# The first load of a layernorm kernel, in one transfer or in three transfers over interleaved partitions

## The chip, the cores and the metric

The kernel runs on one core of a Trainium2 chip. The metric is the time of one execution on the device, in microseconds.

## The reference

```python
z = x + residual                       # (16, 1024, 512) float32
mean = np.mean(z, axis=-1, keepdims=True)
var = np.var(z, axis=-1, keepdims=True)
z_norm = (z - mean) / np.sqrt(var + eps)
out = gamma * z_norm + beta
```

That is 33.5 MB of x, 33.5 MB of the residual and 33.5 MB of output: 100.7 MB through the core's DMA engines, and little arithmetic for each byte.

## The kernel before

Rows of 512 numbers are spread over 128 partitions. A written plan gives the order of the transfers, all issued from SyncE: `x0+8` loads rows 0 to 7 of each partition, `r` is the residual, `o` a store.

```python
PLAN = """
x0+8 r0+8 x8+8 r8+8 x16+16 r16+16 x32+16 r32+16 x48+16
o0+16 r48+16 ...
"""
EARLY = 2
...
    def move(out, in_, s):
        i = nc.sync.dma_start(out=out, in_=in_).then_inc(s, 16)
        if len(first) < EARLY:
            first.append(i.ins)
...
        if kind == "x":
            # (cut: waits for stores, once the buffer is used again)
            move(part(zbuf, Z_ROWS, lo, n), dram(xf, lo, n), sx[loads_x.index((lo, n))])
...
                nc.gpsimd.wait_ge(s[landed[key]], 16)      # GpSimd, ahead of each add
```

At the end of the program the instructions in `first` are moved ahead of the barrier with which all engines begin. So the first two loads, x0 and r0, are issued at once and everything else after the barrier. GpSimd adds, ScalarE takes mean and variance, VectorE normalizes, SyncE stores.

Of the kernel before, what the change touches and what calls it, by code (L numbers as in the profile page):

```python
# [14 lines left out]
Z_ROWS = 64  # L15
# [16 lines left out]
Z_TURNS = Z_ROWS // TURN  # L32


EARLY = 2


@with_exitstack
def kernel(
# [9 lines left out]
    nc = tc.nc  # L49
    P = nc.NUM_PARTITIONS  # L50
    xf = x.flatten_outer_dims()
# [16 lines left out]
    def of_kind(kind):  # L68
        found = [(lo, n) for k, lo, n in moves if k == kind]
        assert sum(n for _, n in found) == total  # L70
        return found

    def dram(t, lo, n):

        b0 = lo - lo % BLOCK
        v = t[P * b0 : P * (b0 + BLOCK), :].rearrange("(p j) d -> p j d", p=P)
        return v[:, lo - b0 : lo - b0 + n, :].rearrange("p a b -> p (a b)")

    zbuf = nc.alloc_sbuf_tensor("zbuf", [P, Z_ROWS * D], FP32)
# [17 lines left out]
    def sem(name):  # L97
        s = nc.alloc_semaphore(name)
        sems.append(s)
        return s  # L100

    loads_x, loads_r, stores = of_kind("x"), of_kind("r"), of_kind("o")
    sx = [sem(f"sx{c}") for c in range(len(loads_x))]
# [13 lines left out]
    def part(buf, size, lo, n):  # L117
        assert lo % size + n <= size
        return buf[:, (lo % size) * D : (lo % size + n) * D]
# [17 lines left out]
    first = []  # L137

    def move(out, in_, s):
        i = nc.sync.dma_start(out=out, in_=in_).then_inc(s, 16)  # L140
        if len(first) < EARLY:
            first.append(i.ins)

    gone = 0
    for kind, lo, n in moves:
        if kind == "x":
            while gone < len(stores) and stores[gone][0] < lo + n - Z_ROWS:
                nc.sync.wait_ge(so[gone], 16)
                gone += 1
            move(part(zbuf, Z_ROWS, lo, n), dram(xf, lo, n), sx[loads_x.index((lo, n))])  # L150
        elif kind == "r":
            if lo + n > R_ROWS:
                last = (lo + n - R_ROWS) // TURN - 1
                nc.sync.wait_ge(s_rstd[last % Z_TURNS], last // Z_TURNS + 1)
            move(part(rbuf, R_ROWS, lo, n), dram(rf, lo, n), sr[loads_r.index((lo, n))])
        else:
            if lo + n > seen:
                nc.sync.wait_ge(s_out, lo + n)
                seen = lo + n
            move(dram(of, lo, n), part(zbuf, Z_ROWS, lo, n), so[stores.index((lo, n))])  # L160
# [9 lines left out]
    landed = {"x": 0, "r": 0}  # L170
    lo = 0
    for n in ADDS:
        for key, loads, s in (("x", loads_x, sx), ("r", loads_r, sr)):
            while landed[key] < len(loads) and loads[landed[key]][0] < lo + n:
                nc.gpsimd.wait_ge(s[landed[key]], 16)  # L175
                landed[key] += 1
        z = part(rbuf, R_ROWS, lo, n)
        nc.gpsimd.tensor_tensor(  # L178
            out=z, in0=part(zbuf, Z_ROWS, lo, n), in1=z, op=ALU.add
        ).then_inc(s_sum[lo // TURN % R_TURNS], 1)  # L180
        lo += n
# [131 lines left out]
```

## Time and profile before

| | before |
|---|---|
| time, median of the first 3 runs | 238.48 us |
| span of the profiled run | 236.7 us |
| busy: DMA queue of SyncE / ScalarE / VectorE / GpSimd | 99.4% / 78% / 75% / 61% |
| first issue, first packets | 0.00 us; 1.02 to 1.49 us |
| first add on GpSimd | 12.29 us |

Read the table from its third row down: one queue is busy all the time. The lines behind it are in the prediction.

### The profile page before, as it was taken

How to read it: one execution, taken by the hardware profiler on the slowest of the kernel's cores; microseconds unless marked ns; L12 is line 12 of the kernel's file. 1: busy time of each engine (PE TensorE's matmuls, PEld its weight loads, DVE VectorE, ACT ScalarE, POOL GpSimd, SP SyncE). 2: the span in 40 equal slices, each digit the busy share in tenths (PEclk: the TensorE clock that was granted, in tenths of full speed). 3: DMA queues.
4: the chain of work that ended last, by engine and by line, in shares of the span. 5: the costliest groups of instructions: out<-in, count | busy, mean ns of one | idle time of the engine just before them, and what ended most of it. 6: DMA issues, size and time to landing. Idle time of an engine off the chain costs nothing.

```text
span 236.7 us, 1000 instructions
## 1 busy us (share of the span) xinstructions
PE 3.8 (2%) x4; PEld 1.2 (0%) x4; DVE 177.2 (75%) x290; ACT 183.8 (78%) x545; POOL 144.0 (61%) x36
## 2 busy tenths in 40 slices
PE   0600000000000000000000000000000000000000
PEld 0100000000000000000000000000000000000000
DVE  0001999629999999599980999809999999999950
ACT  2019997299999996999909998099999999999600
POOL 0098920999799307993079920899799798800000
DMA  8999999999999999999999999999999999999997
GB/s 310 443 426 432 426 443 443 443 443 443 410 388 443 443 443 432 426 393 432 443 443 443 443 438 421 415 421 432 429 424 435 426 432 440 439 432 443 438 390 324
DMA packets 4469, 100.68 MB, mean 425 GB/s; under 512 B 498, under 2 KB 498, under 8 KB 500
## 3 DMA queue, kind: packets, MB, share of 16 engines
q1 hardware_dynamic: 4464, 100.67, 99.4%
q14 instruction: 1, 0.01, 0.0%
q10 hardware_dynamic: 4, 0.00, 0.0%
HBM read 67.11 MB, written 33.55 MB: 425 GB/s over the span
## 4 chain that ended last, share of the span: by engine, by line
ACT 48%; DMA 35%; POOL 6%; DVE 4%; issue 1%; SPq 1%; ACTq 0%; DVEq 0%; POOLq 0%
DMA rbuf<-in_residual_dram 35%; ACT junk_s L211 25%; ACT junk_m L201 21%; POOL rbuf L178 6%; DVE zbuf L239 3%; ACT std L220 2%; DVE zbuf L253 1%; SPq L140 1%; DVE rstd L247 0%; ACTq L194 0%; DVEq L231 0%; POOLq L175 0%; ACTq L199 0%; ACTq L195 0%
## 5 line engine op out<-in xcount | busy, mean ns | idle before, releaser
L178 POOL TENSOR_TENSOR rbuf<-zbuf,rbuf 128x2048 f32<-128x2048 f32 x32 | 143.7, 4521 | 62.2 <-DMA rbuf<-in_residual_dram 60.0
L239 DVE SCALAR_TENSOR_TENSOR zbuf<-rbuf,nm,gamma_p 128x512 f32<-128x512 f32 x128 | 87.1, 743 | 47.8 <-ACT std L220 47.8
L201 ACT ACTIVATE junk_m<-rbuf 128x512 f32<-128x512 f32 x128 | 74.2, 580 | 34.0 <-POOL rbuf L178 33.7
L211 ACT ACTIVATE junk_s<-rbuf,nm 128x512 f32<-128x512 f32 x128 | 88.8, 694 | 1.0
L253 DVE SCALAR_TENSOR_TENSOR zbuf<-zbuf,rstd,beta_p 128x512 f32<-128x512 f32 x128 | 87.1, 744 | 1.1
L211 ACT ACTIVATION_READ_ACCUMULATOR junk_s<-rbuf,nm 128x1 f32 x128 | 23.9, 187 | 0.0
L201 ACT ACTIVATION_READ_ACCUMULATOR junk_m<-rbuf 128x1 f32 x128 | 23.8, 186 | 0.0
L220 ACT ACTIVATE std<-ssq,eps_t 128x4 f32<-128x4 f32 x32 | 9.5, 297 | 1.0
L247 DVE RECIPROCAL rstd<-std 128x4 f32<-128x4 f32 x32 | 5.5, 171 | 0.0
L192 ACT ACT_TABLE_LOAD x1 | 1.3, 1283 | 2.7 <-PEq L60 2.7
L131 PE MATMUL gamma_p<-gb_row,ones 1*128 1x512 f32 x2 | 2.0, 1122 | 6.6 <-DMA gb_row<-in_gamma_dram 6.6
L131 PE MATMUL beta_p<-gb_row,ones 1*128 1x512 f32 x2 | 1.9, 1056 | 0.0
L126 DVE MEMSET ones<- 1x128 f32 x1 | 0.2, 165 | 2.0 <-PEq L60 2.0
L131 PEld LDWEIGHTS beta_p<-gb_row,ones 1*128 1x128 f32 x2 | 0.7, 332 | 1.0 <-DMA gb_row<-in_beta_dram 0.5
L131 PEld LDWEIGHTS gamma_p<-gb_row,ones 1*128 1x128 f32 x2 | 0.5, 306 | 6.6 <-issue 6.6
L294 POOL MEMSET const-float32-0.0<- 128x1 f32 x1 | 0.1, 98 | 0.2 <-issue 0.2
L294 POOL MEMSET const-bfloat16-1.0<- 128x1 bf16 x1 | 0.1, 101 | 0.0
L294 POOL MEMSET const-uint8-127<- 128x1 uint8 x1 | 0.1, 101 | 0.0
L294 POOL MEMSET const-float32-1.0<- 128x1 f32 x1 | 0.1, 98 | 0.0
L127 DVE MEMSET eps_t<- 128x1 f32 x1 | 0.1, 59 | 0.0
## 6 DMA issues: line engine op xcount, KB each, us to landing
zbuf<-in_x_dram SPq DMA_DIRECT2D x6, 4096.0 KB, 28.9
rbuf<-in_residual_dram SPq DMA_DIRECT2D x6, 4096.0 KB, 21.2
out_dram<-zbuf SPq DMA_DIRECT2D x6, 4096.0 KB, 31.0
zbuf<-in_x_dram SPq DMA_DIRECT2D x4, 2048.0 KB, 14.9
rbuf<-in_residual_dram SPq DMA_DIRECT2D x4, 2048.0 KB, 14.0
out_dram<-zbuf SPq DMA_DIRECT2D x3, 2048.0 KB, 22.5
out_dram<-zbuf SPq DMA_DIRECT2D x2, 1024.0 KB, 10.0
gb_row<-in_gamma_dram ACTq DMA_DIRECT2D x1, 2.0 KB
```

The lines of the kernel that those rows point to most:

```text
L126: nc.vector.memset(ones[:, :], 1.0).then_inc(s_const, 1)
L131: nc.tensor.matmul(dest[:, :], ones[:, :], gb_row[:, k * D : (k + 1) * D], start=True, stop=True).then_inc(s_pe, 1)
L140: i = nc.sync.dma_start(out=out, in_=in_).then_inc(s, 16)
L178: nc.gpsimd.tensor_tensor(out=z, in0=part(zbuf, Z_ROWS, lo, n), in1=z, op=ALU.add).then_inc(s_sum[lo // TURN % R_TURNS], 1)
L192: act.preload_act_table_set("sqrt_and_others")
L201: i = act.activation(out=junk_m[k][:, :], in_=part(rbuf, R_ROWS, r, 1), func=ACT.Identity, scale=-inv_d, accum_out=column(nm, r),)
L211: i = act.activation(out=junk_s[k][:, :], in_=part(rbuf, R_ROWS, r, 1), func=ACT.Square, bias=column(nm, r), accum_out=column(ssq, r),)
L220: act.activation(out=column(std, rows[0], TURN), in_=column(ssq, rows[0], TURN), func=ACT.Sqrt, bias=eps_t[:, 0:1], scale=inv_d,).then_inc ...
L239: dve.scalar_tensor_tensor(out=part(zbuf, Z_ROWS, r, 1), in0=part(rbuf, R_ROWS, r, 1), scalar=column(nm, r), in1=gamma_p[:, :], op0=ALU.ad ...
L247: dve.reciprocal(out=column(rstd, rows[0], TURN), in_=column(std, rows[0], TURN)).then_inc(s_rstd[j], 1)
L253: i = dve.scalar_tensor_tensor(out=z, in0=z, scalar=column(rstd, r), in1=beta_p[:, :], op0=ALU.mult, op1=ALU.add,)
L294: nc = _bacc.Bacc("TRN2", target_bir_lowering=False, num_devices=1)
```

## The change

The intent, as far as the edit shows it: give the sixteen DMA engines their first work from a smaller transfer, so that all of them start sooner. The first load, 128 partitions of 16 KB, becomes three: partitions 0, 4, 8, ...; then 2, 6, 10, ...; then the odd ones. All three are issued ahead of the barrier; the residual's first load moves behind it.

```diff
-EARLY = 2
+FIRST = [(0, 4), (2, 4), (1, 2)]
...
-        if len(first) < EARLY:
+        if len(first) < len(FIRST):
...
-            move(part(zbuf, Z_ROWS, lo, n), dram(xf, lo, n), sx[loads_x.index((lo, n))])
+            for a, step in FIRST if lo == 0 else [(0, 1)]:
+                move(
+                    part(zbuf, Z_ROWS, lo, n)[a::step, :],
+                    dram(xf, lo, n)[a::step, :],
+                    sx[loads_x.index((lo, n))],
+                )
...
-                nc.gpsimd.wait_ge(s[landed[key]], 16)
+                pieces = len(FIRST) if key == "x" and landed[key] == 0 else 1
+                nc.gpsimd.wait_ge(s[landed[key]], 16 * pieces)
```

## The prediction

> **What bounds the kernel now.** I read the page's busy line and its three DMA rows first, then the DMA issues, then short windows at the two ends of the span. The page of the kernel before:
>
> ```profile
> PE 3.8 (2%) x4; PEld 1.2 (0%) x4; DVE 177.2 (75%) x290; ACT 183.8 (78%) x545; POOL 144.0 (61%) x36
> ...
> DMA  8999999999999999999999999999999999999997
> ...
> q1 hardware_dynamic: 4464, 100.67, 99.4%
> ```
>
> No compute engine is over 78% busy, while the queue that carries all loads and stores has its packets busy for 99.4% of sixteen engines' span. All 38 inner slices of the DMA row read 9; only the first and the last do not. The chain of work that ended last names ACT for 48% and DMA for 35%, but it cannot outvote this: it follows who released whom, and the queue never ran dry. The end of the SyncE timeline shows why not. The last store of 1 MB is issued at 228.2 us, and these windows (length, busy of PE, PEld, DVE, ACT, POOL, clock, DMA share, GB/s) show what happens after it:
>
> ```profile
> 228.00:230.00 2.00, 0.00 (x0) 0.00 (x0) 0.20 (x1) 0.00 (x0) 0.00 (x0) 1.00 0.99 426
> ...
> 234.00:235.00 1.00, 0.00 (x0) 0.00 (x0) 0.00 (x0) 0.00 (x0) 0.00 (x0) 1.00 1.01 426
> 235.00:236.00 1.00, 0.00 (x0) 0.00 (x0) 0.00 (x0) 0.00 (x0) 0.00 (x0) 1.00 0.26 107
> ```
>
> VectorE is done at 228.2; the queue works at full rate for 7 us more. One megabyte is 2.4 us at 426 GB/s, so the last store could have been issued some 4.5 us later before an engine went idle. Compute has that slack, and the end is: **when the first packet starts, plus the bytes, plus the completion of the last store.** Check: 100.68 MB at the middle's 432 GB/s (window 60 to 220 us) is 233 us, a first packet at about 1.2 us, and slower rates in the opening and at the end make up the rest to 235.5. So a change at the opening can only move the first of these terms, and the opening is where the change is.
>
> The opening, from the timeline and from windows of a tenth of a microsecond:
>
> ```profile
> 0.00 0.38 SPq L140 DMA_DIRECT2D zbuf<-in_x_dram  x1
> ...
> 0.43 0.42 SPq L140 DMA_DIRECT2D rbuf<-in_residual_dram  x1
> 1.92 0.33 SPq L140 DMA_DIRECT2D zbuf<-in_x_dram  x1
> ```
> ```profile
> 1.00:1.10 0.10, 0.00 (x0) 0.00 (x0) 0.00 (x0) 0.00 (x0) 0.00 (x0) 1.00 3.19 655
> 1.10:1.20 0.10, 0.00 (x0) 0.00 (x0) 0.00 (x0) 0.00 (x0) 0.00 (x0) 1.00 3.08 655
> 1.20:1.30 0.10, 0.00 (x0) 0.00 (x0) 0.00 (x0) 0.00 (x0) 0.00 (x0) 1.00 3.12 655
> 1.30:1.40 0.10, 0.00 (x0) 0.00 (x0) 0.00 (x0) 0.00 (x0) 0.00 (x0) 1.00 1.63 328
> 1.40:1.50 0.10, 0.00 (x0) 0.00 (x0) 0.00 (x0) 0.00 (x0) 0.00 (x0) 1.00 1.33 328
> 1.50:1.60 0.10, 0.00 (x0) 0.00 (x0) 0.00 (x0) 0.00 (x0) 0.00 (x0) 1.00 0.00 0
> ```
>
> A packet is counted where it starts, and a packet of this load is one partition's 16 KB, so 655 GB/s over 0.1 us is four packets and 328 is two. Four, four, four, two and two: sixteen engines start their first packet between 1.0 and 1.5 us, mean about 1.21 us. Nothing starts in the next window. The share column gives what these packets took: 3.19 + 3.08 + 3.12 + 1.63 + 1.33 = 12.35, times 0.1 us and 16 engines, over 16 packets, is 1.24 us each. A steady one takes 0.62 us (window 6.9 to 11.9: share 0.99 at 423 GB/s). So the opening costs a latency of 1.0 us after the first issue, a stagger of up to 0.5 us between engines, and a slow first packet.
>
> [...]
>
> **The change part by part.** It removes one load of 2 MB and adds loads of 0.5, 0.5 and 1 MB of the same bytes, before the same barrier. The first load of the residual leaves that place and goes behind the barrier.
>
> Start of the engines: the first piece has 32 descriptors instead of 128. If the stagger of about 0.45 us scales with the count, the last engine starts near 1.1 us instead of 1.45, and the mean moves from 1.21 to about 1.07. Gain 0.14 us in the mean, up to 0.35 us for the last engines. If the whole issue also gets shorter (0.38 us to perhaps 0.25), 0.1 us more. An engine then has two packets of the first piece, 1.24 + 0.62 us, and the second piece is issued near 0.4 us and ready near 1.4: nothing starves.
>
> Added packets: each engine writes two more completions. The trace's 4-byte packets take 9 ns, so 0.02 us of queue time. [...]
>
> Added issues: from the timeline an issue takes 0.33 to 0.51 us and the next starts about 0.05 us later. SyncE reaches the barrier after three issues rather than two, so everything behind it, now at 1.92 us, may come 0.1 to 0.45 us later. The residual's load then issues near 2.2 us instead of 0.43; an engine needs it when its eight x packets are done, near 6.5 us. Gamma and beta are needed by VectorE first at 22.7 us, and the ACT table, loaded from 2.7 to 4.0 us, at 16.8. All hidden.
>
> Waits: the first add starts at 12.29 us, held by the residual, and should start about 0.2 us earlier.
>
> Sum on the path: minus 0.15 to 0.35 for the start, plus 0.02: about minus 0.2 us. 238.48 - 0.2 = **238.3 us**, or 0.1%. I choose the middle, because the end is set by the slowest engine, whose lateness has other sources too.
>
> **The rivals.** First, nothing at all: the stagger at the start may be absorbed where reads and writes mix, since the rate wanders between 388 and 443 GB/s in the slices. For it: such variation is much larger than 0.2 us. Against it: there is no idle gap to absorb it in. That makes 238.5 us, inside the spread of the runs (238.36 to 238.83).
> [...] Eight packets for each engine at half rate would cost up to 8 x 0.61 = 4.9 us, an estimate: 243.2 us, slower by 2%. [...] I give a loss of this kind 7%, at its full size 3%.
> Third, a delayed barrier becomes the wait[...]. It has 4 us in hand; dismissed.
> Fourth, a greater gain: the slow first packets (1.24 us against 0.62) become fast when fewer come at once. That would be at most 0.6 us: 237.7. I see no reason for it, as all sixteen still start together.
>
> **Range and chances.** The centre is 238.3; the runs' spread of 0.2 us either way and a gain from 0 to 0.4 give 237.9 to 238.7 for 8 in 10. Faster by 2% would need 4.8 us, which the opening does not hold: 1%. Slower by 2%: [...]3%. Within 2%: 96%.
>
> **What would show it.** Right: sixteen packets start within about 0.15 us of each other near 1.0 us, the inner slices keep their 9s, the residual's first issue moves to about 2.2 us, the first add to about 12.1, and the end comes about 0.2 us sooner. Wrong: packets of 1.2 us instead of 0.62 throughout the first 10 us[...], a GB/s hole before 7 us, or a first start later than 1.0 us, if a smaller transfer has no earlier start.

Passages of this record that no trace or run of this case shows are cut, and marked. Minus 0.15 to 0.35 us for the start and plus 0.02 for the added packets came to about minus 0.2, so 238.48 - 0.2 = 238.3 us. The second rival: a loss in which the packets of the pieces move at half rate. Its size: an estimate from the trace's 0.61 us for each packet; the 7% and 3% given to it were the author's estimate, for which no trace was shown. The third rival is that the residual's load, late behind the barrier, leaves the engines without work. The "32 descriptors" of the first piece are its 32 packets of 16 KB, one for each partition. The added completions can be counted on the two pages: 498 packets under 512 B before and 530 after, so 32 more, or two for each of sixteen engines.

## The result, and the profile after

The changed kernel took 239.22 us (median of 6 runs, 239.02 to 240.07), the kernel before 238.27 (6 runs, 238.03 to 238.83). Ratios here are the mean time of one kernel's fast runs over that of the other's of the same rounds, so not quite the ratio of the medians: 1.0043, with a 95% interval of 1.0024 to 1.0062. The change is a small loss, clear of noise, where a gain of 0.2 us had been predicted.

Where the time went can be read in four views. The first is the SyncE timeline of the changed kernel (start, duration, instruction; the first two lines, the first and the third piece alone, are from narrower windows):

```profile
0.00 0.55 SPq L140 DMA_DIRECT2D zbuf<-in_x_dram  x1
...
1.22 0.59 SPq L140 DMA_DIRECT2D zbuf<-in_x_dram  x1
...
3.11 0.36 SPq L140 DMA_DIRECT2D rbuf<-in_residual_dram  x1
3.52 0.42 SPq L140 DMA_DIRECT2D zbuf<-in_x_dram  x1
4.00 0.79 SPq L140 DMA_DIRECT2D rbuf<-in_residual_dram  x1
4.83 0.80 SPq L140 DMA_DIRECT2D zbuf<-in_x_dram  x1
5.68 0.67 SPq L140 DMA_DIRECT2D rbuf<-in_residual_dram  x1
```

The issue of 32 strided partitions took 0.55 us; that of all 128 had taken 0.38. The barrier is passed 1.2 us later than before (3.11 against 1.92). And three plain issues at 4.0 to 6.3 us took 0.7 to 0.8 us, where the same issues had taken 0.43 to 0.51.

The second view is windows of a tenth of a microsecond (length, busy of PE, PEld, DVE, ACT, POOL, clock, DMA share, GB/s); a packet counts where it starts, and 164 GB/s is one packet:

```profile
1.20:1.30 0.10, 0.00 (x0) 0.00 (x0) 0.00 (x0) 0.00 (x0) 0.00 (x0) 1.00 0.00 0
1.30:1.40 0.10, 0.00 (x0) 0.00 (x0) 0.00 (x0) 0.00 (x0) 0.00 (x0) 1.00 3.71 819
1.40:1.50 0.10, 0.00 (x0) 0.00 (x0) 0.00 (x0) 0.00 (x0) 0.00 (x0) 1.00 2.12 492
1.50:1.60 0.10, 0.00 (x0) 0.00 (x0) 0.00 (x0) 0.00 (x0) 0.00 (x0) 1.00 1.26 328
1.60:1.70 0.10, 0.00 (x0) 0.00 (x0) 0.00 (x0) 0.00 (x0) 0.00 (x0) 1.00 3.37 819
```

Nothing starts before 1.3 us. In the trace's transfer records the first packets start at 1.32 to 1.89 us, mean 1.53; before it was 1.02 to 1.49, mean 1.20. The smaller piece starts 0.33 us later, not sooner, and the engines are no closer together (0.57 us from first to last against 0.47).

The third view is longer windows, first of the kernel before, then of the changed one:

```profile
1.00:4.00 3.00, 0.00 (x0) 0.00 (x0) 0.17 (x2) 1.28 (x1) 0.00 (x0) 1.00 1.04 350
4.00:8.00 4.00, 1.37 (x2) 0.83 (x3) 0.00 (x0) 0.00 (x0) 0.00 (x0) 1.00 1.01 431
```
```profile
1.00:4.00 3.00, 0.00 (x0) 0.00 (x0) 0.17 (x2) 0.09 (x1) 0.00 (x0) 1.00 0.95 333
4.00:8.00 4.00, 0.15 (x1) 0.18 (x2) 0.00 (x0) 1.20 (x1) 0.00 (x0) 1.00 0.97 353
...
4.50:5.00 0.50, 0.00 (x0) 0.00 (x0) 0.00 (x0) 0.50 (x1) 0.00 (x0) 1.00 0.64 229
...
6.50:7.00 0.50, 0.00 (x0) 0.00 (x0) 0.00 (x0) 0.00 (x0) 0.00 (x0) 1.00 0.60 229
```

The late start costs 17 GB/s over 3 us, which is 0.05 MB or 0.12 us at 431 GB/s. The stretch from 4 to 8 us costs 78 GB/s over 4 us: 0.31 MB or 0.72 us. That is the larger part, and it was not in the prediction at all. Of the packets that start in this stretch, 25 take over 0.7 us in the changed kernel and none before; the longest takes 1.59 us. A low share does not by itself show idle engines, as a packet counts where it starts: the last two windows read alike, but a count of the packets under way at each moment finds idle engines only from 4 to 6 us (3.0 us of one engine's time in all) and all sixteen at work from 6.5 to 7.0. The records do not name the engine, but starts can be matched to ends: three engines end their fourth packet (two of the first piece, two of the second) at 4.48 to 4.65 us and begin the fifth at 5.26, 5.33 and 5.79; a fourth engine stands idle from 4.69 to about 5.09. They have run dry waiting for the third piece, which was issued from 1.22 to 1.81 us.

These gaps are the smaller part of the loss. The stretch costs some 0.7 us of all sixteen engines, about 11 us of one engine's time: 3.1 us are gaps, and 8.1 us are what the 25 slow packets took over the usual 0.61. Only three of the slow packets follow a gap, and 17 of them start after 6 us, when no engine is idle. What they wait for, no record shows.

The fourth view is the first add on GpSimd, which waits for the slowest engine's share of x0 and r0, and the windows at the end of the changed kernel:

```profile
13.99 4.49 POOL L184 TENSOR_TENSOR rbuf<-zbuf,rbuf 128x2048 f32<-128x2048 f32 x1 [13.56 <-DMA rbuf<-in_residual_dram]
```
```profile
235.00:236.00 1.00, 0.00 (x0) 0.00 (x0) 0.00 (x0) 0.00 (x0) 0.00 (x0) 1.00 0.63 262
236.00:237.00 1.00, 0.00 (x0) 0.00 (x0) 0.00 (x0) 0.00 (x0) 0.00 (x0) 1.00 0.30 123
237.00:238.00 1.00, 0.00 (x0) 0.00 (x0) 0.00 (x0) 0.00 (x0) 0.00 (x0) 1.00 0.14 57
```

The first add starts at 13.99 us against 12.29: 1.70 us later, though the sixteen engines together are only 0.9 us behind. The dry spell hits some engines and not others. The kernel ends with them still apart: before, the queue's rate falls off within the window from 235 to 236 us; now it trails off over more than two. The span of the profiled run grew by 1.6 us (238.3 against 236.7), much as the first add did, and that run was one of the longer ones (239.64 us); the median grew by 0.95.

The bound itself is the same: the queue is still 98.8% busy by the page, VectorE ends at 230.5 us, and the queue works for 7 us after it.

### The profile page after: what moved, and what is told of

The parts are those of the page before. It is cut to its first block, busy times and chain, and to the rows that moved or that the text cites. A ratio compares the mean times of both kernels' runs of the same rounds, so it can differ in the third digit from the quotient of the medians.

```text
span 238.3 us, 1002 instructions
## 1 busy us (share of the span) xinstructions
PE 3.7 (2%) x4; PEld 1.1 (0%) x4; DVE 177.2 (74%) x290; ACT 183.8 (77%) x545; POOL 144.0 (60%) x36
## 3 DMA queue, kind: packets, MB, share of 16 engines
q1 hardware_dynamic: 4496, 100.67, 98.8%
## 4 chain that ended last, share of the span: by engine, by line
ACT 48%; DMA 35%; POOL 6%; DVE 4%; issue 1%; SPq 1%; ACTq 0%; DVEq 0%; POOLq 0%
DMA rbuf<-in_residual_dram 35%; ACT junk_s L217 25%; ACT junk_m L207 21%; POOL rbuf L184 6%; DVE zbuf L245 3%; ACT std L226 2%; SPq L140 1%; DVE zbuf L259 1%; DVE rstd L253 0%; ACTq L200 0%; DVEq L237 0%; POOLq L181 0%; ACTq L205 0%; ACTq L201 0%
```

## The experiments

Sixteen runs of fifteen kernels, in four batches. In the expectations, "lag" is the number of bytes that the queue had moved by a given time in the kernel before, less those in this run, divided by 0.43 MB/us. It is worked out from the transfer records; in the changed kernel it is 0.16 us at 4 us and 0.94 us at 10 us. The table gives for each run what was read from its trace: first packets, packets of over 0.7 us (for each 16 KB) among those that start from 4 to 8 us, the start of the first add, and the time.

| run | first packets, us | slow packets | first add, us | time, us | ratio to before |
|---|---|---|---|---|---|
| before | 1.02 to 1.49 | 0 | 12.29 | 238.01 to 238.27 (medians of the batches) | 1 |
| the change | 1.32 to 1.89 | 25 | 13.99 | 239.22 | 1.0043 |
| f4, the change again | 1.32 to 1.80 | 21 | 13.86 | 239.60 | 1.0057 |
| e1, residual early too | 1.32 to 2.12 | 27 | 13.79 | 239.47 | 1.0056 |
| e2, one whole load early | 1.00 to 2.03 | 0 | 12.44 | 238.03 | 0.9994 |
| e5, three by columns | 1.00 to 1.26 | 0 | 12.55 | 238.54 | 1.0019 |
| e6, three blocks | 1.05 to 1.83 | 50 of 50 | 17.12 | 242.55 | 1.0183 |
| e3, four quarters | 1.35 to 2.00 | 22 | 13.92 | 239.66 | 1.0071 |
| e7, a later load in three | 1.02 to 1.93 | 0 | 12.34 | 238.10 | 1.0004 |
| e4b, two halves (e4 is alike, with one packet of 0.79 us) | 1.33 to 2.15 | 0 | 12.52 | 238.45 | 1.0017 |
| e8, residual in three too | 1.31 to 2.01 | 24 | 14.11 | 239.35, one look | |
| e9, odd half first | 1.33 to 2.16 | 0 | 12.77 | 238.41 | 1.0016 |
| e10, residual before odd half | 1.32 to 2.02 | 9 | 13.60 | 239.81 | 1.0074 |
| e11, third piece waits | 1.32 to 1.90 | 17 | 14.03 | 239.81, one look | |
| f1, quarter, half, quarter | 1.35 to 2.30 | 1 | 12.84 | 239.22, one look | |
| f2, 16 rows | 1.32 to 2.19 | 0 | (other plan) | 238.43, one look | |
| f3, 4 rows | 1.32 to 1.93 | 27 | (other plan) | 240.31, one look | |

### First batch: the residual's place, or the pieces?

The first theory, L, was that the residual and all behind it came too late. The rival, P, was that the pieces are slow by themselves.

**e1** puts the residual's load ahead of the barrier again, behind the three pieces.

```diff
-        if len(first) < len(FIRST):
+        if len(first) < 4:
```

> The three strided pieces as in the change, but the residual's first load follows them ahead of the barrier (four issues in the opening). Theory L (late residual: what the changed kernel loses between 4 and 8 us comes from issuing the residual's load, and all behind it, after the barrier at 3.1 us): the slow stretch goes, only the 0.15 us of the late first packets stays, about 238.4. Theory P (the pieces: their partition steps make the issue and the packets slow by themselves): the slow stretch stays, about 239.2 or a little more, as the barrier moves to about 3.6 us.

Measured: 239.47 us, ratio 1.0056 (1.0040 to 1.0072), 27 slow packets. Theory L falls: with the residual early the slow stretch is as large.

**e2** is the kernel before with only the whole first load of x ahead of the barrier.

```diff
-EARLY = 2
+EARLY = 1
```

> The kernel before with one load in the opening: the whole first load of x, with the residual's behind the barrier. Theory L: part of the loss appears, 238.5 to 239.0, with packets of over 0.7 us between 3 and 8 us. Theory P: no loss, 238.3 as before, and all packets after the first near 0.62 us; the residual then issues near 1.5 us, well ahead of need.

Measured: 238.03 us, ratio 0.9994 (0.9981 to 1.0007), no slow packet. The residual's place alone costs nothing, which confirms that step of the prediction.

**e5** cuts the first load into three transfers of all 128 partitions, by rows within each partition.

```diff
-FIRST = [(0, 4), (2, 4), (1, 2)]
+FIRST = [(0, 2), (2, 2), (4, 4)]       # first row, rows
-                    part(zbuf, Z_ROWS, lo, n)[a::step, :],
-                    dram(xf, lo, n)[a::step, :],
+                    part(zbuf, Z_ROWS, lo + a, rows),
+                    dram(xf, lo + a, rows),
```

> The first load of x in three transfers of all 128 partitions: rows 0-1, 2-3 and 4-7 of each partition, so the same bytes for each piece as in the change, no partition step, packets of 4, 4 and 8 KB. Theory L: as in the change, 239.0 to 239.3, as the residual is as late. Theory P: each issue takes about 0.4 us and not 0.55, the first packets start at 1.0 us, no slow stretch from the stride, 238.2 to 238.6.

Measured: 238.54 us (238.33 to 239.98), ratio 1.0019 (1.0006 to 1.0032). The issues took 0.38, 0.42 and 0.43 us, the first packets started at 1.00 us, and no packet between 4 and 8 us was slow. So three transfers ahead of the barrier, with the residual behind it, do no harm in the opening where there is no partition step. What little this run lost it lost later: at 50 us its lag was 0.03 us, at 100 us 1.16. That was the run of 239.98, the slowest of its five.

**e6** takes the same three sizes as blocks of neighbouring partitions: `[(0, 32), (32, 64), (64, 128)]` and `[a:step, :]` in place of `[a::step, :]`.

> The same three sizes in whole blocks of partitions: 0-31, 32-63, 64-127, no step. If the stride is what makes an issue long, each takes about 0.4 us; if the partition count (under 128), 0.55 to 0.6. [...]packets of these pieces take 1.2 us and the first load lands some 2 to 4 us later, 240 to 242 us[...].

Measured: 242.55 us, ratio 1.0183 (1.0170 to 1.0196). The window from 4 to 8 us:

```profile
4.00:8.00 4.00, 0.00 (x0) 0.00 (x0) 0.00 (x0) 0.81 (x1) 0.00 (x0) 1.00 0.95 205
```

The share is 0.95 and the rate 205 GB/s: every engine is busy and a 16 KB packet takes 1.21 us on average, twice the ordinary time, and so on until the eight packets of the first load are through. Why these blocks of neighbouring partitions move at half the rate, no record shows. The issues took 0.40, 0.41 and 0.53 us and the first packet started at 1.05, so neither a count below 128 nor three transfers make the first issue long and the start late: the step does. The changed kernel looks different: between 4 and 8 us it has idle engines, and 61 of its 86 packets take no more than 0.7 us.

### Second batch: slow descriptors, or the odd half?

Theory G: descriptors of a strided load, one for each partition, are made slowly, at about 38 ns each, which is an estimate: 0.61 us for each packet, over sixteen engines. No view shows a descriptor being made; the runs can only test what would follow. Theory C: the 64-row piece moves slowly by itself, the 32-row ones do not.

**e3** cuts the first load into quarters only: `FIRST = [(0, 4), (2, 4), (1, 4), (3, 4)]`.

> The first load in four pieces of 32 partitions (every fourth from 0, 2, 1 and 3); the 64-row piece is gone. Theory G (the descriptors of a load with a partition step are made slowly, at about 38 ns each, so the engines run dry or restart around the third piece and the plain issues behind it are held up): the same slow stretch between 4 and 8 us and held-up issues of 0.7 to 0.9 us, 239.2 to 239.6. Theory C[...]: no slow stretch, 238.3 to 238.6.

Measured: 239.66 us, ratio 1.0071 (1.0054 to 1.0087), 22 slow packets, plain issues of 0.76 and 0.64 us. Theory C falls: no 64-row piece is needed.

**e7** leaves the first load whole and cuts a later one, x16, which has some 15 us of work queued ahead of it.

```diff
-            for a, step in FIRST if lo == 0 else [(0, 1)]:
+            for a, step in FIRST if lo == 16 else [(0, 1)]:
```

(The early count is 2 as before, and the wait for three pieces moves to that load.)

> The first load whole as before; instead the third load of x (16 rows, 4 MB, issued near 2.8 us with about 15 us of work queued ahead) is cut into the same three strided pieces. Theory G: the slow making of descriptors is hidden behind the queue; all packets of these pieces keep their ordinary time, and only the issues behind are held up: 238.0 to 238.4. Theory C: the odd half moves at a lower rate wherever it stands, some 1 to 2 us over its 2 MB: 239 to 240.

Measured: 238.10 us, ratio 1.0004 (0.9987 to 1.0021), all packets at their ordinary time (this load's are of 32 KB and take 1.21 us, as before). Here, where the strided pieces are not waited for, they move at full rate. So the prediction's second rival, these pieces at half rate, is out.

**e4** and, timed, **e4b** cut the load into halves: `FIRST = [(0, 2), (1, 2)]`.

> The first load in two pieces of 64 partitions, even and odd. Theory G: the same 128 strided descriptors, so about the same loss, 238.9 to 239.6, with the dry spot again between 4 and 8 us. Theory C: [...]packets are slow from the first ones on and the loss doubles, about 240.

> The two halves again, now timed: one look gave 238.85. If its opening lag of 0.2 us is all, 238.3 to 238.5; if the transition from loads to the first store near 67 us takes 0.5 us more of it, as that look had it, 238.7 to 239.0. The opening must again show no packet over 0.7 us after the second of each engine.

Measured: one look 238.85; timed 238.45 us, ratio 1.0017 (1.0000 to 1.0034). The SyncE timeline and the window of the timed run:

```profile
0.00 1.18 SPq L140 DMA_DIRECT2D zbuf<-in_x_dram  x2
2.48 0.36 SPq L140 DMA_DIRECT2D rbuf<-in_residual_dram  x1
...
3.37 0.45 SPq L140 DMA_DIRECT2D rbuf<-in_residual_dram  x1
```
```profile
4.00:8.00 4.00, 0.45 (x1) 0.48 (x2) 0.00 (x0) 0.57 (x1) 0.00 (x0) 1.00 0.96 407
8.00:12.00 4.00, 3.29 (x4) 0.67 (x3) 0.00 (x0) 0.00 (x0) 0.00 (x0) 1.00 1.04 446
```

The two issues take 1.18 us, 0.55 and 0.58 with a gap, so each is as slow as in the change, and the first packets start as late. But no engine runs dry: the plain issues keep their 0.36 to 0.49 us, no packet in the stretch is over 0.7 us, and the 407 of one window is made good by the 446 of the next (packets are counted at their starts). The lag stays at 0.20 us. The same 128 strided rows in two transfers do no more than start late, so theory G falls as well: it predicted the dry spot here too. This run also shows the cost of the late start by itself: a lag of 0.20 us at 10 us, and about 0.4 us in the time (0 to 0.8 by the interval).

**e8** cuts the residual's first load into the same three pieces.

> The residual's first load is cut into the same three strided pieces as well, behind the barrier. Theory G: twice as many slow descriptors; if one costs clearly more than the 38 ns at which the 16 engines use them up, the loss about doubles, to 240 or more, with slow packets until 10 us or later; if it costs about 38 ns, the loss hardly grows, 239.2 to 239.8. Theory C: a second slow stretch where the odd half of the residual is moved, near 10 us, and 240.

Measured: 239.35 us in one look, lag 1.13 us at 10 us against 0.94 (and 1.06 in f4 below). Three more strided transfers add little; they are issued well before they are wanted, which may be why. That was within what G allowed for its cheaper case; e4b decided against G.

### Third batch: the third transfer

In every slow run so far engines ran dry ahead of the third transfer, which followed two quarters. Theory S: only about two strided transfers are in the making, and a third waits until an earlier one has landed.

**e9** changes the order: `FIRST = [(1, 2), (0, 4), (2, 4)]`, the odd half first.

> The three pieces in another order: the 64 odd partitions first, then the two quarters. Theory S (only about two strided transfers are in the making at a time, and the rows of a third one start to reach the engines only some 0.8 us after an earlier one has landed): the first piece keeps each engine busy until about 4.2 us, the third is wanted only near 5.5 us, and it comes by then: little or no slow stretch, byte lag at 10 us 0.2 to 0.4 us, 238.3 to 238.9. Theory G (each strided row costs about 38 ns whatever the order): the eighth packet of each engine is as late as in the change, lag at 10 us 0.8 us or more, 239.0 to 239.5.

Measured: 238.41 us, ratio 1.0016 (0.9999 to 1.0033), lag 0.25 us, no slow packet, no issue held up. The same three pieces, with the large one first, cost only the late start. The interval overlaps that of the change (1.0024 to 1.0062) but not that of its repeat, f4 (1.0040 to 1.0074). The barrier is passed at 3.12 us here too, and ScalarE loads gamma, beta and its table from 3.13 to 5.2 us as in the change, so the place of that work, a rival that had not been named, does not make the slow stretch.

**e10** issues the two quarters, then the residual whole, then the odd half.

> The two quarters, then the residual's first load whole, then the odd half (behind the barrier). If only the third strided transfer is late, and a plain one is not, the residual fills the gap: no dry spot at 4.4 us, the odd half hides behind the residual's 5 us, lag at 10 us near 0.2 us, 238.3 to 238.9. If any third transfer behind two strided ones is late, the residual's packets show the same 0.8 to 1.6 us at 4.2 to 6.3 us, and the lag is 0.9 us, 239.0 to 239.4.

Measured: 239.81 us, ratio 1.0074 (1.0058 to 1.0091), lag 0.57 us. Most engines went on without a gap, but three ran dry at about 4.45 us and began the residual only at 5.0 to 5.3. So a plain transfer behind two quarters comes late too, on some engines. The expectation of a filled gap was wrong. The other branch did not fit in its numbers: the lag is smaller than its 0.9 us, and the time is longer than its 239.4, no shorter than the change's. So the lag alone does not set the time.

**e11** lets SyncE wait for the first quarter's landing ahead of the third piece.

```diff
+                if k == 2:
+                    nc.sync.wait_ge(s_a, 16)
```

(The first quarter has a semaphore of its own, on which GpSimd waits too.)

> The change, but the odd half has to wait on SyncE until the first quarter has landed (about 3.2 us), so it is issued near 3.4 us instead of 1.2. Theory S: its rows reach the engines hardly later than in the change, as they waited for that anyway; lag at 10 us 0.8 to 1.2 us and the plain issues behind it take about 0.45 us, none 0.7 to 0.9. Theory G or any theory in which the rows of the odd half were being made since 1.8 us: they come 1 to 2 us later than in the change, and the lag grows to 1.6 us or more, about 240.

Measured: 239.81 us in one look, lag 1.72. Theory S's branch (a lag of 0.8 to 1.2) did not come. The time and lag are in the range expected of G, but not by its mechanism. The SyncE timeline and windows of that run:

```profile
3.98 0.48 SPq L141 DMA_DIRECT2D zbuf<-in_x_dram  x1
```
```profile
4.40:4.80 0.40, 0.00 (x0) 0.00 (x0) 0.00 (x0) 0.15 (x1) 0.00 (x0) 1.00 0.02 0
4.80:5.20 0.40, 0.27 (x1) 0.30 (x2) 0.00 (x0) 0.00 (x0) 0.00 (x0) 1.00 0.00 0
5.20:5.60 0.40, 0.40 (x1) 0.20 (x1) 0.00 (x0) 0.00 (x0) 0.00 (x0) 1.00 2.09 451
```

The odd half is issued at 3.98 us; no packet of a load starts from 4.3 to 5.2 us, and then all sixteen engines begin at 5.25 to 5.91 us and go on with hardly a gap. Fifteen of the 17 slow packets are such first ones. Behind nothing else, the odd half takes 1.27 to 1.93 us from issue to first packet, just what the first quarter takes at the start. In the changed kernel the same piece, issued at 1.22 us, had not reached three engines 4.0 us later.

### Fourth batch: what the lateness is tied to

**f1** is quarter, half, quarter: `FIRST = [(0, 4), (1, 2), (2, 4)]`.

> Order quarter, odd half, quarter. If two quarters ahead are what delays the third transfer: no slow stretch, lag at 10 us 0.25 us, no later issue held up over 0.6 us. If one quarter is enough, some plain issue behind the barrier is held for 0.7 to 0.9 us; the engines have six packets before the third piece, so the lag may still be only 0.3 to 0.6 us.

Measured: 239.22 us in one look, but with one slow packet, no issue over 0.5 us behind the barrier and a lag of 0.29 us: no slow stretch. At the end one engine was about 1 us behind the others; why is open.

**f2** makes the first load 16 rows (`x0+16 r0+8 r8+8`), so that its packets are 32 KB. **f3** makes it 4 rows (`x0+4 r0+8 x4+4 x8+8`), with packets of 8 KB. The rest is the change.

> The change with a first load of 16 rows, so packets of 32 KB and 1.2 us: the first quarter lands near 4.2 us instead of 3.2. If the delay of the third transfer is tied to that landing, the held-up issues end near 5.8 us for the first of them instead of 4.8, and the odd half comes near 5.5 us or later. If it is tied to a time after the start, they end at 4.8 us as in the change, and no engine runs dry, as its first four packets last until 6.3 us.

> The change with a first load of 4 rows, packets of 8 KB and 0.3 us: the first quarter lands near 2.4 us. Tied to the landing: the odd half arrives near 3.4 to 4.2 us and held-up issues end near 4.0 us. Tied to a time after the start: it arrives at 4.2 to 5.8 us as in the change, and the engines stand dry from 3.0 us on, a lag of 1.5 us or more.

Measured: f2 238.43 us in one look, no slow packet, no issue over 0.5 us; f3 240.31 us in one look, lag 1.87 us, 27 slow packets, and plain issues of 0.60 and 1.14 us from 4.5 to 6.3 us. For the held-up issues neither expectation fits: in f2 none is held up at any time, in f3 they are held up later than in the change and not sooner. For the odd half's arrival, f3 fits the branch of the landing: engines that had run dry began it at 3.5 to 4.1 us (3.4 to 4.2 expected), against 5.1 to 5.8 in the change. So a fixed time is out. Theory S failed in e11 and on the held-up issues; whether the arrival has to do with the landing of the first quarter stays open, as in f2 no engine wanted the third piece early enough to tell. What does sort the runs is when the engines want the third transfer. With 16 KB packets and two quarters ahead they want it at about 4.3 us (the change, e1, e3, e8, e10, f4): late. With 8 KB packets they want it at about 3.0 us (f3): worst. With a half among the first two they want it at about 5.5 us or later (e4b, e9, f1), and with 32 KB packets at about 7.1 us (f2): in time. Plain issues held up for over 0.6 us appear only in the runs in which engines ran dry.

**f4** repeats the change.

> The changed kernel again. If its opening is a property of the program, the lag at 10 us is again 0.8 to 1.1 us, with held-up issues of 0.7 to 0.9 us and a time of 239.0 to 239.4; if it was chance, the opening differs.

Measured: 239.60 us (239.13 to 239.83), ratio 1.0057 (1.0040 to 1.0074), lag 1.06 us, 21 slow packets, issues of 0.84 and 0.65 us; the time is above the 239.4 expected. The slow opening belongs to the program and is not chance; its details vary, as does the time.

## Why the prediction was wrong

**The bound: right.** The queue sets the end, and only its start and its evenness were open to this change. The window views at the two ends carried that, and they also show the loss. But "a change at the opening can only move the first of these terms" was too narrow: it also changed how long the packets took.

**The start of the engines: wrong in sign.** The step was "if the stagger of about 0.45 us scales with the count, the last engine starts near 1.1 us", with an issue of "perhaps 0.25" us. Measured: first packets at 1.32 to 1.89 us instead of 1.02 to 1.49, and an issue of 0.55 us instead of 0.38. Every run that begins with a strided piece has its first packet at 1.31 to 1.35 us, whether of 32 or 64 partitions; every run without has it at 1.00 to 1.05 (e2, e5, e6, e7). I had taken the cost of an issue to fall with the number of partitions and had no figure for a partition step, as the kernel before has none. Of the predicted 0.2 us gain a loss of about 0.4 us remained, which e4b (1.0017) and e9 (1.0016) show by themselves, though the interval of each reaches down to 1.000.

**"The second piece is issued near 0.4 us and ready near 1.4: nothing starves": the step that failed most.** It holds for the second piece and fails for the third. Two quarters give an engine four packets, which last until about 4.4 us; the third piece reached some engines only at 5.3 to 5.8. This term was zero in my sum. The stretch from 4 to 8 us cost 0.72 us of the queue's work, and more on the slowest engine, for which the first add waits 1.7 us longer. About a quarter of the 0.72 us is engines that starved; the rest is 25 packets of 0.7 to 1.6 us, where the prediction had 0.62 us for every packet after an engine's first. Two of its own signs of being wrong came: a first start later than 1.0 us and a hole in the rate before 7 us.

**The added issues: mis-sized, but hidden.** The barrier came 1.2 us later and not 0.1 to 0.45. By e2 the residual's place behind it costs nothing, and by e1 putting it back gains nothing.

**The rivals.** The rival at half rate was rightly held to be unlikely: e7 has the same pieces at full rate (1.21 us for 32 KB), and the steady half rate that was feared came only with the blocks of e6 (1.21 us for 16 KB). A small, sure loss from the pieces' own making was not among the rivals, so the range stopped at 238.7 us and missed.

**What stays open.** Why the third transfer is so late in the change, although the same piece alone takes 1.3 to 1.9 us, is not settled. Shown are the conditions: it follows two strided quarters, it is late whether strided or plain (e10), the delay is not a fixed cost for each strided row (e4b, e9), and it shows only where an engine has by then nothing else to do. Why the other engines' packets are slow around it, the larger part of the stretch's loss, is open too; apart from e6, whose packets are slow from the start, more than one slow packet came only in runs with such gaps. What becomes of the third transfer between its issue and its first packets, no view here tells. Nor is the opening loss the whole of the end's: between 66 and 75 us, where the first store follows the loads, the lag of the change fell from 0.92 to 0.62 us and that of the first run with halves rose from 0.20 to 0.73. The link between the uneven engines at the start and at the end is read from the traces of the two kernels and was not tried by itself.

## What to carry to other kernels

A transfer cut up to start sooner must start sooner: measure the issue and the first packet of the cut shape, here a partition step made the first issue 0.17 us longer and the first packet 0.3 us later. Each early piece has to last until the next one reaches the engines, here until 5.3 to 5.8 us where two quarters lasted until about 4.4; if anything is cut, try the large piece in front (1.0016 in e9, against 1.0043 and 1.0057 with it last). Under a queue that is never idle, look at when the slowest engine gets its first loads done, and not only at the sum of bytes: here the first add's delay (1.7 us) came nearer to the growth of the span (1.6 us) than the sum of bytes did (0.9 us), though no run tried this by itself.

## What was measured of the transfers

- From a plain load's issue to its first packet: 1.02 us after the start of the issue, 0.64 us after its end (before). With a partition step it was 1.32 us after the start and 0.77 after the end (the change).
- A partition step: as the first issue of the program it took 0.54 to 0.56 us, for 32 and 64 partitions alike, against 0.38 to 0.40 without the step. What stands ahead counts as well: the odd half issued at 3.98 us with SyncE idle before it took 0.48 us (e11), and a plain load right behind three strided pieces took 0.58 (e1).
- The blocks of neighbouring partitions in e6 moved at half the rate: their packets took 1.21 us instead of 0.61, and the kernel 1.8% longer. Interleaved halves kept the ordinary time (e4b: no packet from 4 to 8 us over 0.7 us), and so did interleaved quarters and the odd half in e7 (1.21 us for 32 KB). How rows are dealt to engines, no record shows.
- A third small transfer reached the engines 1.3 to 1.9 us after its issue where the engines had nothing else ahead of it (e11), and up to 4.6 us after it behind two strided quarters (the change).
